# A new table of durations and delays for the list scheduler of a one-core decoder trunk

## The chip, the cores and the metric

One core of one Trainium2 chip runs the whole program in one launch. The metric is the device time of an execution in microseconds (us). Each time belongs to a run; the profile is that of one execution.

## The reference, cut to what matters

Two layers work on 256 tokens of width 1024, all in float32. Each layer adds four results to the residual `h`:

```
h += 0.5 * SwiGLU_1(rms(h))                          # width 2816
h += W_out [ A | B | C ](rms(h) @ W_in)
     # A: gated DeltaNet, 4 heads x 128: short causal conv on q/k/v, per-head decay, chunks
     #    t_inv = triangular_solve(eye + lower, eye); u = t_inv (v beta); w = t_inv (k beta exp(gc))
     # B: dilated sliding-window attention, 4 heads x 64;  C: chunked causal spatial gating
h += CrossAttn(rms(h), rms(mem))                     # 4 heads, 256 memory tokens
h += 0.5 * SwiGLU_2(rms(h))
```

After the second layer one more RMS norm gives the output. What is computed, and by which instructions, is the same before and after the change; only their order differs.

## The kernel before, in words

The function `trunk` (L421) does not issue instructions. It describes them, through small wrapper classes (`Tensor`, `Scalar`, `Vector`, `Queue`, L317 to L420), to an object of the class `Plan` (L136). Each wrapper gives `Plan.add` the engine, the operands and a rough duration. `Plan.schedule` (L191) then simulates the five engines with these durations. It always places the instruction that can start first; among those of one engine that can start at the same time it takes the one with the longest way to the end of the program ("rank"). `HOPS` are the delays from the end of an instruction on one engine to the start of one that depends on it on another. A tile gets one of the slots of its tag when its first instruction is placed, and for the tags in `KEEP` the last free slot is kept for the oldest waiting tile. `Plan.emit` (L298) issues the list, every instruction at L313. So each engine runs its instructions in the order that the simulation found, and the table of durations and delays sets that order. The loads of the weights keep the order of the program text.

The numerics are float32 by splitting: a weight piece `wr` [128, 1024] is rounded by ScalarE into `wh`, and VectorE (now and then GpSimd) writes the rest into `wl`. TensorE multiplies `wh` and `wl` with operands `X` (the gained residual) or `S`, into banks called `pg`; these matmuls have 512 or 256 columns and make up most of TensorE's work.

The small work stands in other tiles. `ps` are PSUM banks of everything that is no weight product. Statistics of a norm (`Stats`, `rsqrt`, `newton`): squares of the residual summed on GpSimd into `t`; TensorE sums over partitions (`ps<-one,t`); VectorE and GpSimd make the inverse root `rc` (`rv`, `rna`); TensorE spreads it over rows (`ps<-one,rch`), and VectorE stores it as `rb`. The mixing part (`mixing`) has the convolution in `xs` and `q`, the decays in `g8` (L830 to L848: three narrow matmuls with `g8` on one side, then per token tile four matmuls that spread it over 128 partitions), and the triangular inverse (L953 to L1003). For the inverse each of the two token tiles has a matrix in `uc` and its transposed blocks in `tc`. A level of it is: four 64x64 matmuls `ps<-tc,Mb`, two ScalarE copies into `Q`, four 64x64 matmuls `ps<-Q,uc`, then on VectorE two subtractions `tc<-tc,ps` and four block transposes `uc<-tc`, each over another group of 32 partitions. Four such levels follow each other, then a last one over `ng`, and two more products. The chain is long and each step is short, so the order decides what stands beside it.

Of the kernel before, what the change touches and what calls it, by code (L numbers as in the profile page):

```python
# [32 lines left out]
# columns of the constants that depend on shapes alone  # L33
# [10 lines left out]
# per-layer columns (small)  # L44
# [5 lines left out]
# per-layer columns (used in the mixing part)  # L50
# [8 lines left out]
class View:  # L59
    """A slice of a planned tile: where it lies, and how to take it from the real tile."""  # L60
# [75 lines left out]
class Plan:  # L136
    """Instructions in program order, placed on the engines by a list schedule (longest way to
    the end first) with rough durations in us, then issued in that order."""

    HOPS = {("ACT", "DVE"): 0.13, ("ACT", "GP"): 0.17, ("ACT", "PE"): 0.3, ("DVE", "ACT"): 0.13,  # L140
            ("DVE", "GP"): 0.16, ("DVE", "PE"): 0.7, ("GP", "DVE"): 0.06, ("GP", "PE"): 0.2,
            ("GP", "ACT"): 0.1, ("PE", "ACT"): 0.2, ("PE", "DVE"): 0.2,
            ("DVE", "DVE"): 0.13, ("ACT", "ACT"): 0.145, ("GP", "GP"): 0.1}
    DMA_ISSUE, DMA_DONE = 1.6, 1.8
    SLACK = 0.0
    KEEP = ("pg", "ps", "wh", "wl")  # their last free slot waits for the oldest tile
# [14 lines left out]
    def add(self, eng, method, args, kw, outs, ins, dur, table=None):  # L161
        i = len(self.ops)
        op = dict(i=i, eng=eng, method=method, args=args, kw=kw, dur=dur, table=table, prio=self.boost,
                  tiles=[], preds={}, succs=[])
# [21 lines left out]
    def hop(self, a, b):  # L186
        if a["eng"] == "DMA":
            return self.DMA_DONE
        return self.HOPS.get((a["eng"], b["eng"]), 0.0)

    def schedule(self):  # L191
        ops = self.ops
        for o in reversed(ops):
            o["tail"] = o["dur"] + max([ops[j]["tail"] + self.hop(o, ops[j]) for j in o["succs"]],
                                       default=0.0)
# [18 lines left out]
        dma_next, table = 0, None  # L214
# [6 lines left out]
        order, left = [], len(ops)  # L221

        def slot_time(o):
            """when slots for the tiles that o begins are free (None: not known yet)."""
            t = 0.0
            for x in o["tiles"]:
                if x.slot is None:
                    f = slots[x.tag]
                    best = min(f)
                    if x.tag in self.KEEP and queue[x.tag][0] is not x:  # L230
                        best = sorted(f)[1]
                    if best == float("inf"):
                        return None
                    t = max(t, best + (self.DMA_ISSUE if best and o["eng"] == "DMA" else 0.0))
            return t

        while left:
            best = None
            for e, lst in ready.items():
                if not lst:  # L240
                    continue
                if e == "DMA":
                    lst = [o for o in lst if o["i"] == dmas[dma_next]]
                cands = []
                for o in lst:
                    st = slot_time(o)
                    if st is not None:
                        cands.append((max(o["at"], st, free[e]), o))
# [4 lines left out]
                for t, o in cands:  # L253
                    if t > t0 + self.SLACK:
                        continue
                    k = o["rank"]
                    if e == "ACT" and o["table"] and table and o["table"] != table:
                        k -= 2.0
                    k = (k, -o["i"])
# [8 lines left out]
            dur = o["dur"]  # L268
            if e == "ACT" and o["table"] and o["table"] != table:
                dur += 1.28  # L270
                table = o["table"]
            if e == "DMA":
                dma_next += 1
            ready[e].remove(o)
            o["start"] = t
            end = free[e] = t + dur
            done = end + (self.DMA_DONE if e == "DMA" else 0.0)
            for x in o["tiles"]:
                if x.slot is None:
                    f = slots[x.tag]  # L280
                    x.slot = f.index(min(f))
# [3 lines left out]
                x.done = max(x.done, done)  # L285
                if not x.left:
                    slots[x.tag][x.slot] = x.done + 0.2
# [29 lines left out]
class Tensor:  # L317
# [3 lines left out]
    def matmul(self, o, lhsT, rhs, start, stop):  # L321
        n, m = o.free(), lhsT.shape[1]
        if lhsT.tile.dt == F32R and rhs.tile.dt == F32R:
            dur = max(n / 2.4, m / 1.2) / 1000 + 0.002
        else:
            dur = 2 * max(n / 1.2, m * 0.76) / 1000 + 0.004
        self.plan.add("PE", "matmul", (o,), dict(lhsT=lhsT, rhs=rhs, start=start, stop=stop),
                      [o], [lhsT, rhs], dur)

    def transpose(self, o, i, ident):  # L330
        self.plan.add("PE", "transpose", (o, i, ident), {}, [o], [i, ident], 0.11)


class Scalar:
    SETS = {AF.Exp: "exp", AF.Silu: "silu", AF.Tanh: None}

# [3 lines left out]
    def copy(self, o, i):  # L340
        self.plan.add("ACT", "copy", (o, i), {}, [o], [i], 0.09 + 0.83e-3 * o.free())

    def activation(self, o, i, f, **kw):
        n = o.free()
        dur = 0.09 + 0.83e-3 * n
        ins, outs = [i], [o]
        for k in ("scale", "bias"):
            if isinstance(kw.get(k), View):
                ins.append(kw[k])
                dur += 0.09  # L350
        if "accum_out" in kw:
            outs.append(kw["accum_out"])
            dur += 0.1
        table = "exp" if f in (AF.Exp, AF.Tanh) else "silu" if f == AF.Silu else None
        self.plan.add("ACT", "activation", (o, i, f), kw, outs, ins, dur, table)


class Vector:
# [3 lines left out]
    def _add(self, method, args, kw, outs, ins, fast=False, ap=0):  # L362
        n = max(outs[0].free(), ins[0].free()) if ins else outs[0].free()
        if self.eng == "GP":
            dur = 0.14 + 2.13e-3 * n
        else:
            dur = 0.068 + (0.52e-3 if fast else 1.04e-3) * n + 0.06 * ap
        if kw.get("op") == ALU.pow:
            dur = 0.3 + 0.165 * n
        if method == "memset":  # L370
            dur = 0.06 + 0.5e-3 * n
        if method == "reciprocal":
            dur = 0.07 + 6.3e-3 * n
        self.plan.add(self.eng, method, args, kw, outs, ins, dur)
# [35 lines left out]
class Queue:  # L410
# [3 lines left out]
    def dma_start(self, o, i):  # L414
# [3 lines left out]
        self.plan.add("DMA", "dma_start", (o, i), {}, [o], [i], max(n * 4 / 360e3, 0.1))  # L418


def trunk(tc, xT, memT, w, w2, ca_d, cb_d, sm_d, fin_d, lb_d, out):  # L421
    plan = Plan(tc)
    PE, ACT, DVE, GP, SY = Tensor(plan), Scalar(plan), Vector(plan, "DVE"), Vector(plan, "GP"), Queue(plan)
    with ExitStack() as ctx:
# [24 lines left out]
        # ---- residual and constants  # L449
# [46 lines left out]
        def wchunk(engs=(None, None), cut=1):  # L496
            """next weight chunk as two pieces of 1024 columns, each in two parts."""
# [11 lines left out]
        def mm3(o, wt, c, x, first, last):  # L509
            """o += W[:, c:c+128]^T x with W and x each in two parts."""  # L510
# [17 lines left out]
        def mm3x(o, x, t, wt, ws, first, last):  # L528
            """o += x[:, token tile t]^T W[:, ws]."""
# [16 lines left out]
        def mmp(o, a, i, sa, b, j, sb, first, last):  # L546
            """o += a[:, i, sa]^T b[:, j, sb] with both in two parts."""
# [4 lines left out]
        def gained(src, g, slot, dve=False):  # L552
            """two parts of src * g (g per partition)."""
# [19 lines left out]
        class Stats:  # L573
# [47 lines left out]
        class Norm:  # L621
            """operands and statistics of the next norm, one residual tile at a time."""
# [74 lines left out]
        def proj_add(ops, order, nxt):  # L697
            """h += W^T ops, two column tiles of W a chunk."""
# [10 lines left out]
        def pair(x, engs=(None, None)):  # L709
            """next chunk of two column tiles against x -> one bank [128, 2, 256]."""  # L710
# [7 lines left out]
        def xstat512(x):  # L718
            """two chunks of 4 k x 512 columns -> banks [tokens, 512] of both token tiles."""
# [11 lines left out]
        def xstat256(x, pieces=None, n=T):  # L731
            """8 k x n columns in two pieces -> banks [tokens, n] of both token tiles."""
# [48 lines left out]
        # ---- parallel mixing  # L781
        def mixing(l, norm, nxt, xm):
# [5 lines left out]
            # step sizes and decays  # L788
# [580 lines left out]
```

## Time and profile before

| | us |
|---|---|
| median of 3 runs | 1298.19 |
| lowest and highest run | 1297.84 and 1536.4 |
| span of the profiled execution | 1297.0 |
| TensorE (PE) busy in the span | 1257.6 |
| VectorE (DVE) busy | 985.8 |
| ScalarE (ACT) busy | 700.3 |
| GpSimd (POOL) busy | 267.3 |

The runs' time takes in a little more than the span: 0.8 to 1.2 us for the two lower runs. Of a matmul the trace shows a start and a modelled end, so two neighbours overlap; the distance from start to start tells what one costs. A float32 matmul that is not in the rounded form stands in the trace as two records. The number in square brackets behind a row is the time that the engine was idle ahead of it, and what ended it. "PEclk" is the granted clock of TensorE, 1.00 for 2.4 GHz and 0.50 for 1.2 GHz.

### The profile page before, as it was taken

The numbers are of one execution on the slowest core, as the hardware profiler recorded it, in microseconds if no ns is written. First come the engines' busy times: TensorE is split into PE (matmuls) and PEld (weight loads), VectorE is DVE, ScalarE is ACT, GpSimd is POOL, SyncE is SP. The second block draws the span as 40 slices with busy tenths as digits, with TensorE's granted clock in tenths as the row PEclk, the third lists the DMA queues.
The fourth block names the chain that finished last, engine by engine and source line by source line (L and its number), as shares of the span: only waits on it lengthen the run. The fifth ranks groups of instructions, "written<-read, shape, count | busy, mean of one in ns | idle before, by whom it ended". The sixth has DMA issues, their size and how long they took to land.

```text
span 1297.0 us, 21998 instructions
## 1 busy us (share of the span) xinstructions
PE 1257.6 (97%) x8376; PEld 1134.8 (87%) x8376; DVE 985.8 (76%) x1645; ACT 700.3 (54%) x1208; POOL 267.3 (21%) x281
## 2 busy tenths in 40 slices
PE   6999999899999999999999999989999999999997
PEld 5888889888999988888988888988989989888886
DVE  7777887997776777777777787779976767777764
ACT  5655645556544555555455664464564454565542
POOL 4000443603250230001200001435034305000021
PEclk9999999999999999999999999989999999999998
DMA  6556564323445345555555565532235453455551
GB/s 216 190 184 218 206 226 150 111 82 109 156 171 184 114 165 193 195 179 194 189 172 187 185 215 207 202 115 98 82 105 194 168 178 120 171 187 195 187 196 72
DMA packets 60873, 216.26 MB, mean 167 GB/s; under 512 B 7136, under 2 KB 7520, under 8 KB 60640
## 3 DMA queue, kind: packets, MB, share of 16 engines
q1 hardware_dynamic: 60768, 214.86, 48.5%
q8 instruction: 66, 1.08, 0.3%
q14 instruction: 39, 0.32, 0.1%
HBM read 213.78 MB, written 1.05 MB: 166 GB/s over the span
## 4 chain that ended last, share of the span: by engine, by line
PE 85%; DVE 8%; issue 3%; POOL 2%; ACT 1%; DMA 0%; POOLq 0%; DVEq 0%; SPq 0%; ACTq 0%
PE pg L313 78%; PE ps L313 8%; DVE wl L313 2%; DVE S L313 2%; POOL t L313 1%; DVE q L313 1%; ACT S L313 1%; DVE X L313 1%; ACT wh L313 1%; DVE tc L313 0%; DVE rna L313 0%; DVE ab L313 0%; DVE uc L313 0%; DMA one<-xT 0%; DVE po L313 0%
## 5 line engine op out<-in xcount | busy, mean ns | idle before, releaser
L313 PE MATMUL pg<-X,wh 128*128 128x512 f32 (+1 forms) x2240 | 642.4, 356 | 8.4 <-DVE X L313 8.4
L313 DVE TENSOR_TENSOR wl<-wr,wh 128x1024 fp32r<-128x1024 f32 (+1 forms) x386 | 483.3, 1260 | 194.4 <-ACT wh L313 190.1
L313 ACT CAST wh<-wr 128x1024 fp32r<-128x1024 f32 (+2 forms) x398 | 413.0, 1045 | 386.1 <-PE pg L313 227.2
L313 PE MATMUL pg<-X,wl 128*128 128x256 f32 x1824 | 484.7, 284 | 1.4 <-DVE wl L313 1.4
L313 PEld LDWEIGHTS pg<-X,wh 128*128 128x128 f32 x2240 | 384.4, 190 | 55.0 <-ACT wh L313 7.1
L313 PE MATMUL pg<-S,wh 128*128 128x256 f32 (+1 forms) x1560 | 383.5, 326 | 0.0
L313 PEld LDWEIGHTS pg<-X,wl 128*128 128x128 f32 x1824 | 345.4, 189 | 20.7 <-DVE wl L313 3.1
L313 PE MATMUL pg<-S,wl 128*128 128x256 f32 x1088 | 300.2, 281 | 1.3 <-DVE wl L313 1.3
L313 PEld LDWEIGHTS pg<-S,wh 128*128 128x128 f32 x1560 | 258.8, 188 | 24.7
L313 PEld LDWEIGHTS pg<-S,wl 128*128 128x128 f32 x1088 | 204.7, 188 | 4.3 <-DVE wl L313 1.8
L313 POOL TENSOR_TENSOR t<-one 128x256 f32<-128x256 f32 x70 | 55.2, 790 | 641.2 <-DVE one L313 635.9
L313 POOL TENSOR_TENSOR t<-t,t 128x256 f32<-128x256 f32 x68 | 89.7, 1320 | 4.7
L313 DVE TENSOR_TENSOR t<-t,pg 128x256 f32<-128x256 f32 x204 | 83.0, 414 | 5.9 <-ACT t L313 5.9
L313 ACT COPY t<-pg 128x256 f32<-128x256 f32 x204 | 73.4, 367 | 23.6 <-PE pg L313 21.4
L313 ACT ACTIVATE t<-t 128x256 f32<-128x256 f32 x88 | 36.7, 418 | 52.5 <-DVE t L313 52.4
L313 DVE SCALAR_TENSOR_TENSOR X<-one,one,X 128x256 fp32r<-128x256 f32 x64 | 55.9, 879 | 0.0
L313 PE MATMUL ps<-S,S 128*128 128x256 f32 (+4 forms) x384 | 51.2, 288 | 2.1 <-ACT S L313 1.2
L313 DVE TENSOR_TENSOR S<-t,S 128x256 fp32r<-128x256 f32 x88 | 37.0, 423 | 20.3 <-ACT S L313 20.3
L313 DVE TENSOR_TENSOR t<-t,rbh 128x256 f32<-128x256 f32 x116 | 49.6, 429 | 1.8 <-POOL t L313 0.2
L313 PEld LDWEIGHTS ps<-S,S 128*128 128x128 f32 (+2 forms) x384 | 44.4, 178 | 6.1 <-ACT S L313 1.7
L313 ACT CAST S<-t 128x256 fp32r<-128x256 f32 x88 | 35.0, 407 | 27.3 <-DVE t L313 27.3
L313 PE MATMUL pg<-wh,X 128*128 128x264 f32 (+2 forms) x192 | 45.4, 321 | 0.0
(178 smaller groups left out, 1011.8 us busy)
## 6 DMA issues: line engine op xcount, KB each, us to landing
wr<-w SPq DMA_DIRECT2D x390, 512.0 KB, 3.3
wr<-w SPq DMA_DIRECT2D x4, 528.0 KB, 3.3
S<-memT SPq DMA_DIRECT2D x8, 256.0 KB, 6.5
lb<-lb SPq DMA_DIRECT2D x2, 704.0 KB, 4.7
one<-cb SPq DMA_DIRECT2D x1, 1248.0 KB, 7.1
one<-xT SPq DMA_DIRECT2D x4, 256.0 KB, 5.1
wr<-w SPq DMA_DIRECT2D x4, 256.0 KB, 5.3
out<-S SPq DMA_DIRECT2D x3, 256.0 KB, 2.4
```

Source lines behind the costliest of these rows:

```text
L313: getattr(self.engines[o["eng"]], o["method"])(*[real(a) for a in o["args"]], **{k: real(a) for k, a in o["kw"].items()})
```

## The change

The scheduler's table is replaced. Delays between engines become shorter, above all to TensorE; the time that an engine is occupied (`dur`) and the time until the result can be read (`lat`) are two numbers; TensorE's kinds of matmul carry a cost of switching from one to the other; VectorE and GpSimd exclude each other in the simulation where both read two operands from the SBUF; the tag `t` joins `KEEP`; and the way to the end counts `lat` and the delay instead of the duration. The core of the diff:

```diff
-    HOPS = {("ACT", "DVE"): 0.13, ("ACT", "GP"): 0.17, ("ACT", "PE"): 0.3, ("DVE", "ACT"): 0.13,
-            ("DVE", "GP"): 0.16, ("DVE", "PE"): 0.7, ("GP", "DVE"): 0.06, ("GP", "PE"): 0.2,
...
-    KEEP = ("pg", "ps", "wh", "wl")  # their last free slot waits for the oldest tile
+    HOPS = {("PE", "ACT"): 0.037, ("PE", "DVE"): 0.037, ("ACT", "PE"): 0.054, ("DVE", "PE"): 0.054,
+            ("GP", "PE"): 0.054, ("ACT", "GP"): 0.079, ("DVE", "GP"): 0.079, ("GP", "GP"): 0.079,
+            ("PE", "PE"): -0.2}
+    HOP, ISSUE, FLIGHT, FEED = 0.034, 0.47, 1.75, 385e3
+    KEEP = ("pg", "ps", "wh", "wl", "t")
...
+                        if o["kind"] == "2":
+                            t = max(t, lock["GP" if e == "DVE" else "DVE"])
...
         if lhsT.tile.dt == F32R and rhs.tile.dt == F32R:
-            dur = max(n / 2.4, m / 1.2) / 1000 + 0.002
+            kind, dur = "r", max(0.4525e-3 * n, m / 1.2e3) + 0.0025
+            lat = 0.165 + 0.4525e-3 * n
...
     def copy(self, o, i):
-        self.plan.add("ACT", "copy", (o, i), {}, [o], [i], 0.09 + 0.83e-3 * o.free())
+        lat = (0.153 if i.tile.psum else 0.193) + 0.835e-3 * o.free()
+        self.plan.add("ACT", "copy", (o, i), {}, [o], [i], lat - 0.095, lat)
...
         if self.eng == "GP":
-            dur = 0.14 + 2.13e-3 * n
+            lat, over = 0.19 + 1.67e-3 * n, 0.04
+            if n >= 1024:
+                lat = 2.38
         else:
-            dur = 0.068 + (0.52e-3 if fast else 1.04e-3) * n + 0.06 * ap
+            lat, over = (0.155 if mem else 0.145) + (0.52e-3 if fast else 1.042e-3) * n + 0.06 * ap, 0.08
+            two |= fast and n > 64
...
+        self.plan.add(self.eng, method, args, kw, outs, ins, lat - over, lat,
+                      kind="2" if two or (self.eng == "GP" and views) else None)
```

Three places show what it moves. In names such as `ps_488_2565` the middle number is the tile's number in the program text, the same before and after; the last one tells when the tile was first used.

Place 1, TensorE around the decays `g8` in the first layer, before:

```order
L313 MATMUL pg_523_2458<-X_405_1975,wl_522_2439 128x256
L313 MATMUL ps_582_2558<-q_493_2338 128x128
L313 MATMUL ps_582_2558<-q_495_2346 128x128
L313 MATMUL ps_582_2558<-q_504_2435 128x128
L313 MATMUL ps_582_2558<-q_506_2444 128x128
L313 MATMUL ps_488_2565<-one9_11_1360,g8_484_2556 128x128 x4
L313 MATMUL ps_485_2572<-g8_484_2556,one9_11_1360 128x8
```

The same products after:

```order
L355 MATMUL pg_534_2561<-X_433_2129,wl_530_2509 128x256
L355 MATMUL pg_545_2574<-X_355_1737,wl_541_2581 128x256
L355 MATMUL ps_485_2599<-g8_484_2592,one9_11_1331 128x8
L355 MATMUL ps_485_2599<-g8_484_2592,one9_11_1331 128x4 x2
L355 MATMUL pg_545_2574<-X_366_1745,wh_540_2563 128x256 x2
...
L355 MATMUL pg_545_2574<-X_422_2039,wh_540_2563 128x256 x2
L355 MATMUL ps_488_2623<-one9_11_1331,g8_484_2592 128x128 x4
```

Before, the products with `g8` follow the transposes `ps_582` with no weight product between; after, the rest of `pg_523`, `pg_534` and the start of `pg_545` stand ahead of them, 23.6 us of matmuls by the spacing of their kinds.

Place 2, VectorE in the triangular inverse of the first layer (`tc_576`, `uc_575` are of the first token tile, `tc_586`, `uc_585` of the second), before:

```order
L313 TENSOR_TENSOR tc_576_77<-tc_576_77,ps_592_2828 64x4x32 x2
L313 STREAM_TRANSPOSE uc_575_2733<-tc_576_77 32x4x32 x4
L313 SCALAR_TENSOR_TENSOR q_547_2823<-xs_546_2378,one6_6_65,q_547_2823 128x256
...
L313 TENSOR_TENSOR wl_666_2901<-wr_664_2700,wh_665_2864 128x1024
L313 TENSOR_TENSOR tc_576_77<-tc_576_77,ps_598_2891 64x4x32 x2
L313 STREAM_TRANSPOSE uc_575_2733<-tc_576_77 32x4x32 x4
```

And after:

```order
L355 TENSOR_TENSOR tc_576_77<-tc_576_77,ps_592_3262 64x4x32 x2
L355 STREAM_TRANSPOSE uc_575_3103<-tc_576_77 32x4x32 x4
L355 TENSOR_TENSOR tc_586_85<-tc_586_85,ps_595_3268 64x4x32 x2
L355 STREAM_TRANSPOSE uc_585_3140<-tc_586_85 32x4x32 x4
L355 TENSOR_TENSOR qnqa_569_3270<-qnqa_569_3270,qrq_568_3247 128x8
L355 TENSOR_TENSOR S_722_3173<-S_722_3173,S_721_3162 128x512
L355 TENSOR_TENSOR tc_576_77<-tc_576_77,ps_598_3304 64x4x32 x2
L355 STREAM_TRANSPOSE uc_575_3103<-tc_576_77 32x4x32 x4
```

Before, the two token tiles' levels were spread between convolution and weight work; after, they alternate and stand nearly back to back. From `ps_592` to the last transposes of `uc_585` VectorE has 56 instructions of the chain's own (16 subtractions, 36 block transposes, 4 copies) and 13 others. On TensorE the same stretch holds 20 groups of four 64x64 matmuls and, between them, 17 matmuls of 512 columns with few others; before, the groups stood between the products `pg_556`, `pg_534`, `pg_670` and others of the projection. The second layer looks the same, with 24.7 us of VectorE work by the spacing of its kinds. Over the whole program the changes from a 64x64 group to another kind of product or back fall from 82 to 63.

Place 3, TensorE around the statistics of the second FFN's norm in the first layer (`ps_1037`), before:

```order
L313 MATMUL pg_1027_5312<-X_1016_5290,wh_1022_5238 128x512
L313 MATMUL pg_1027_5312<-X_1016_5290,wl_1023_5255 128x256
L313 MATMUL pg_1027_5312<-X_1019_5325,wl_1023_5255 128x256
L313 MATMUL ps_1037_5341<-one5_5_146,t_981_5061 128x1 x2
L313 MATMUL pg_1035_5344<-X_980_5066,wh_1030_5314 128x512
L313 MATMUL pg_1028_5348<-X_980_5066,wh_1025_5276 128x512
```

After:

```order
L355 MATMUL pg_1027_5314<-X_1019_5326,wl_1023_5257 128x256
L355 MATMUL pg_1035_5342<-X_980_5064,wh_1030_5316 128x512
L355 MATMUL pg_1035_5342<-X_980_5064,wl_1031_5329 128x256
L355 MATMUL pg_1035_5342<-X_983_5101,wh_1030_5316 128x512
L355 MATMUL pg_1027_5314<-X_1019_5326,wh_1022_5240 128x512
L355 MATMUL pg_1035_5342<-X_983_5101,wl_1031_5329 128x256
L355 MATMUL ps_1037_5349<-one5_5_120,t_981_5059 128x1 x2
```

Five weight products more stand ahead of the statistics after. The other norms' statistics move in the same way.

Beside these places, the transposes of the DeltaNet output (`ps_757`, `ps_760`, and `ps_2135`, `ps_2138` in the second layer) stand between pieces of `pg_769` (and its like) after, where they followed each other before. ScalarE loads a function table 14 times in place of 11. The order of the loads on SyncE is unchanged, and so is the end of the program.

## Rows read from the trace of the kernel before

**Rows 1.** The page: busy time, share of the span and instructions of each engine.
```profile
PE 1257.6 (97%) x8376; PEld 1134.8 (87%) x8376; DVE 985.8 (76%) x1645; ACT 700.3 (54%) x1208; POOL 267.3 (21%) x281
```

**Rows 2.** The waits of TensorE: us in total, times, longest.
```profile
PE pg L313 <- DVE X L313: 8.4, 3, 6.9
PE pg L313 <- DVE wl L313: 3.9, 6, 1.2
PE ps L313 <- DVE rch L313: 3.8, 3, 1.6
PE ps L313 <- POOL t L313: 3.5, 7, 1.1
PE ps L313 <- DVE S L313: 3.5, 6, 0.9
...
PE ps L313 <- DVE tc L313: 1.3, 2, 0.7
...
PE ps L313 <- POOL Mb L313: 0.9, 2, 0.7
```

**Rows 3.** Windows: length; PE, PEld, DVE, ACT, POOL busy (instructions); PEclk, DMA share, GB/s.
```profile
230.00:234.00 4.00, 1.74 (x16) 1.57 (x15) 3.79 (x12) 1.31 (x3) 2.64 (x2) 1.00 0.46 155
260.00:280.00 20.00, 20.00 (x198) 17.47 (x196) 19.03 (x54) 10.25 (x25) 2.47 (x8) 1.00 0.24 80
868.00:870.00 2.00, 2.00 (x13) 2.00 (x11) 1.12 (x2) 1.52 (x2) 1.20 (x1) 0.54 0.46 180
870.00:874.00 4.00, 4.00 (x20) 4.00 (x20) 1.33 (x4) 2.11 (x7) 0.00 (x0) 0.50 0.02 4
874.00:876.00 2.00, 2.00 (x15) 2.00 (x14) 2.00 (x8) 1.78 (x4) 1.13 (x2) 0.75 0.00 0
```

**Rows 4.** Timeline of TensorE (start, duration) at the decays of each layer.
```profile
233.86 1.13 PE L313 MATMUL ps<-one,g 128*128 128x128 f32 x8 [2.27 <-issue]
...
867.51 1.02 PE L313 MATMUL ps<-one,g 128*128 128x128 f32 x6 [2.32 <-DVE g L313]
```

**Rows 5.** Timeline of TensorE: weight products of 512 and 256 columns in turn.
```profile
600.04 0.39 PE L313 MATMUL pg<-S,wh 128*128 128x512 f32 x1
600.27 0.28 PE L313 MATMUL pg<-S,wl 128*128 128x256 f32 x1
600.39 0.39 PE L313 MATMUL pg<-S,wh 128*128 128x512 f32 x1
```

**Rows 6.** Timelines of VectorE, GpSimd and TensorE around the first inverse root of the mixing part.
```profile
207.75 2.33 DVE L313 SCALAR_TENSOR_TENSOR rna<-rv,rch 128x2 f32<-128x2 f32 x1 [0.82 <-POOL rch L313]
...
207.69 2.37 POOL L313 TENSOR_TENSOR wl<-wr,wh 128x1024 fp32r<-128x1024 f32 x1
...
210.53 0.71 PE L313 MATMUL ps<-one,rch 128*128 128x128 f32 x4 [1.07 <-DVE rch L313]
```

**Rows 7.** Timeline of TensorE: one 64x64 group and the weight products behind it.
```profile
255.64 0.65 PE L313 MATMUL ps<-tc,Mb 128*64 128x64 f32 x8 [0.69 <-DVE tc L313]
256.22 0.38 PE L313 MATMUL pg<-X,wl 128*128 128x256 f32 x1
256.44 0.40 PE L313 MATMUL pg<-X,wh 128*128 128x256 f32 x2
```

**Rows 8.** Timelines of VectorE and ScalarE in the triangular inverse.
```profile
254.91 0.58 DVE L313 TENSOR_TENSOR tc<-tc,ps 64x128 f32<-64x128 f32 x2
255.52 1.25 DVE L313 STREAM_TRANSPOSE uc<-tc 32x128 f32<-32x128 f32 x4
256.81 0.64 DVE L313 SCALAR_TENSOR_TENSOR q<-xs,one,q 128x256 f32<-128x256 f32 x1
...
278.94 0.69 DVE L313 TENSOR_TENSOR S<-ps,beta 128x512 f32<-128x512 f32 x1
279.55 1.22 DVE L313 TENSOR_TENSOR wl<-wr,wh 128x1024 fp32r<-128x1024 f32 x1
...
256.94 1.28 ACT L313 ACT_TABLE_LOAD   x1
```

More of the change, by code (lines that the diff above doesn't have):

```diff
@@ L159, with add @@
     boost = 0.0
-    def add(self, eng, method, args, kw, outs, ins, dur, table=None):
+    def add(self, eng, method, args, kw, outs, ins, dur, lat, table=None, kind=None):
         i = len(self.ops)
-        op = dict(i=i, eng=eng, method=method, args=args, kw=kw, dur=dur, table=table, prio=self.boost,
-                  tiles=[], preds={}, succs=[])
+        op = dict(i=i, eng=eng, method=method, args=args, kw=kw, dur=dur, lat=lat, table=table, kind=kind,
+                  prio=self.boost, tiles=[], preds={}, succs=[])
         for views, wr in ((ins, False), (outs, True)):
@@ L213, in schedule @@
                     queue[x.tag].append(x)
-        dma_next, table = 0, None
+        dma_next, table, kind, feed = 0, None, None, 0.0
+        lock = {"DVE": 0.0, "GP": 0.0}
         dmas = [o["i"] for o in ops if o["eng"] == "DMA"]
@@ L221, in schedule @@
         order, left = [], len(ops)
+        turn = None
+        if fixed:
+            turn = {e: [o for o in fixed if o["eng"] == e] for e in self.engines}
+            place = {e: 0 for e in self.engines}
+            seq = {}
+            for o in fixed:
+                for x in o["tiles"]:
+                    if x not in seq.setdefault((x.tag, x.was), []):
+                        seq[x.tag, x.was].append(x)
         def slot_time(o):
@@ L228, in slot_time, with switch @@
                     f = slots[x.tag]
-                    best = min(f)
-                    if x.tag in self.KEEP and queue[x.tag][0] is not x:
-                        best = sorted(f)[1]
+                    if fixed:
+                        if seq[x.tag, x.was][0] is not x:
+                            return None
+                        best = f[x.was]
+                    else:
+                        best = min(f)
+                        if x.tag in self.KEEP and queue[x.tag][0] is not x:
+                            best = sorted(f)[1]
                     if best == float("inf"):
                         return None
-                    t = max(t, best + (self.DMA_ISSUE if best and o["eng"] == "DMA" else 0.0))
+                    t = max(t, best)
             return t
+        def switch(o):
+            k = o["kind"]
+            if kind == "r" and k[0] == "f":
+                return 0.091
+            if kind and kind[0] == "f" and k == "r":
+                return 0.2 if kind == "fs" else 0.023
+            return 0.0
         while left:
@@ L243, in schedule @@
                     lst = [o for o in lst if o["i"] == dmas[dma_next]]
+                elif fixed:
+                    lst = [o for o in lst if o is turn[e][place[e]]]
                 cands = []
@@ L258, in schedule @@
                         k -= 2.0
+                    if e == "PE" and switch(o):
+                        k -= self.HOLD
                     k = (k, -o["i"])
@@ L273, in schedule @@
                 dma_next += 1
+                feed = max(feed, t + self.FLIGHT) + lat
+                lat = feed - t
+            if e == "PE":
+                t += switch(o)
+                kind = o["kind"]
+            if o["kind"] == "2":
+                lock[e] = t + dur
             ready[e].remove(o)
+            if fixed:
+                place[e] += 1
             o["start"] = t
-            end = free[e] = t + dur
-            done = end + (self.DMA_DONE if e == "DMA" else 0.0)
+            free[e] = t + dur
+            end = o["end"] = t + lat
             for x in o["tiles"]:
@@ L280, in schedule @@
                     f = slots[x.tag]
-                    x.slot = f.index(min(f))
+                    x.slot = x.was if fixed else f.index(min(f))
                     f[x.slot] = float("inf")
@@ L362, in _add @@
     def _add(self, method, args, kw, outs, ins, fast=False, ap=0):
-        n = max(outs[0].free(), ins[0].free()) if ins else outs[0].free()
+        views = [v for v in ins if isinstance(v, View)]
+        n = max(outs[0].free(), views[0].free()) if views else outs[0].free()
+        mem = [v for v in views if not v.tile.psum and v.free() > 1]
+        two = len(mem) > 1
         if self.eng == "GP":
-            dur = 0.14 + 2.13e-3 * n
-        else:
-            dur = 0.068 + (0.52e-3 if fast else 1.04e-3) * n + 0.06 * ap
+            lat, over = 0.19 + 1.67e-3 * n, 0.04
+            if n >= 1024:
+                lat = 2.38
+        else:
+            lat, over = (0.155 if mem else 0.145) + (0.52e-3 if fast else 1.042e-3) * n + 0.06 * ap, 0.08
+            two |= fast and n > 64
         if kw.get("op") == ALU.pow:
-            dur = 0.3 + 0.165 * n
+            lat = 0.38 + 0.165 * n
         if method == "memset":
-            dur = 0.06 + 0.5e-3 * n
+            lat, over, two = 0.1 + 0.8e-3 * n, 0.0, False
         if method == "reciprocal":
-            dur = 0.07 + 6.3e-3 * n
-        self.plan.add(self.eng, method, args, kw, outs, ins, dur)
+            lat = 0.14 + 6.3e-3 * n
+        self.plan.add(self.eng, method, args, kw, outs, ins, lat - over, lat,
+                      kind="2" if two or (self.eng == "GP" and views) else None)
     def tensor_tensor(self, o, a, b, op):
```

54 lines of the change are left out of this document (27 added, 27 removed).

## The prediction

> **What bounds the kernel now.** I read the page first: TensorE is busy for 1257.6 of 1297.0 us and no other engine comes near [rows 1]. So 39.4 us are all that TensorE is idle, and the time can only fall by what its waits, its changes between kinds of product, or a low clock give back. The list of its waits comes next [rows 2]. The 8.4 us for `X` are the start of the program (6.9 of it before the first matmul) and the tail is unchanged, so neither is in play. What remains in play is short and spread out: 3.9 us for `wl`, 3.8 for `rch`, 3.5 for `t` on GpSimd, 3.5 for `S`, 2.2 for `tc` and `Mb`, and the two waits for the decays, 2.27 and 2.32 [rows 4]. The windows [rows 3] then show two things that the list of waits does not. First, in the mixing part VectorE is nearly full, 19.03 of 20 us at 260 to 280 us, while TensorE is at 20.00: the two engines are close to each other there, so an order that bunches VectorE's work makes TensorE wait. Second, after the idle time ahead of 867.51 TensorE runs at a granted clock of 0.54, 0.50 and 0.75 until 876 us, though it is busy throughout.
>
> **The sum.** It is made against the profiled execution, whose span of 1297.0 stands 1.2 us below the median of the runs; I add the sum to the median.
>
> *Decays (place 1).* Before, TensorE had nothing to do until VectorE had finished the small chain to `g8` (VectorE 3.79 of 4 us busy at 230 to 234 [rows 3]). After, 23.6 us of weight products stand there, against 17.1 us of VectorE work up to `g8`. Both waits go: 2.27 + 2.32 = -4.6. The cover would have to shrink by 6.5 us before any wait comes back.
>
> *Clock in the second layer.* With that idle time gone the half-clock stretch has no cause. At the granted clocks it lost 2 x 0.46 + 4 x 0.50 + 2 x 0.25 = 3.4 us of TensorE's full speed [rows 3]: -3.4. In the first layer the same wait left the clock at 1.00, so nothing is to be had there.
>
> *Statistics (place 3).* Five products more stand ahead of the sums: three of 512 columns at 0.23 us (600.04 to 600.27) and two of 256 at 0.12 (600.27 to 600.39) [rows 5], together 0.93. The wait at this place was the longest, 1.1, of the seven that make 3.5 us [rows 2]. The others moved alike, and four fifths of the sum should go: -2.8, with ends of 0 (the products wait for their own `wh`) and -3.5.
>
> *First inverse root of the mixing part.* At 207.75 a VectorE operation on two columns took 2.33 us, exactly while GpSimd formed a `wl` for 2.37 us [rows 6]; TensorE then waited 1.07 for `rch`. After, that `wl` comes behind the operation, because the slot of its `wh` comes free later. But fewer products cover the root too (14 of `pg_460` and one other, before 22), so I keep 0.3 us of the wait. Two layers, 2 x 0.8: -1.6, with ends 0 and -2.2.
>
> *Output transposes.* They stand between weight products after; of the six waits for `S`, 3.5 us with 0.9 as the longest [rows 2], the four at these transposes go: -2.5, with ends 0 and -3.5. The rest, in cross attention, keeps its order.
>
> *`wl`.* Of 3.9 us [rows 2] I take -1.4: the places ahead of the mixing part and behind it have more products in front of them. The ends are 0 and -3.9; the loads on SyncE are issued in the same order, so nothing new queues there.
>
> *Changes of kind.* A 256-column product after a 64x64 group costs 0.22 us (256.22 to 256.44) where it costs 0.12 elsewhere [rows 5, 7]; I take 0.09 to 0.10 for each direction. There are 19 fewer changes: -1.8.
>
> *Triangular inverse (place 2).* This is the term on the other side, and the largest. On VectorE one level of one token tile takes 254.91 to 256.81 = 1.90 us: two subtractions at 0.31 and four transposes at 0.32 [rows 8]. The new order has eight of these (15.2), four more transposes (1.3), four copies (an estimate of 0.8) and 13 other instructions: one `wl` at 1.2, four 512-wide at 0.6 (278.94 to 279.55), the rest narrow, some 1.8; 5.4 in all. Together 22.7 us. TensorE has for the same stretch 20 groups of 64x64 at 0.47 (8 records; 255.64 to 256.22, less one change) = 9.4, 17 products at 0.23 = 3.9, some 0.8 of other work and about 24 changes = 2.2: 16.3 us. The two alternating tiles keep VectorE busy all through, so TensorE waits for the difference, 6.4 us; in the second layer 24.7 against 19.0, 5.7. That is +12.1 in many pieces of 0.3 to 0.7 us, and 2.2 us of `tc` and `Mb` waits before go into it: +9.9. The ends for a layer are 0 (VectorE runs ahead, or the products next in line fill in) and 16 (the tiles do not alternate, and the 9.4 us of groups come on top).
>
> The Trainium skill ("VectorE: DVE Perf Modes", section "Two Vector instructions with no wait between them") says that an instruction whose first input from a memory starts in another group of 32 partitions than that of the instruction before starts only when all earlier ones have finished. The four transposes of a tile go over four such groups, and they take 0.32 us from start to start, no less than the 0.30 that each lasts [rows 8]. The new table gives VectorE 0.08 us of overlap on every instruction, 0.21 for such a transpose; by the table the wait would be about 1 us a layer and the sum some 10 us lower; by the rule the order cannot change the 0.32, and the sum stands.
>
> *The rest.* ScalarE loads three more tables at 1.28 us [rows 8]. It is 54% busy [rows 1], and its casts stay ahead of VectorE's `wl`; I cost them at nothing. One falls into the chain of the first layer ahead of a copy to `Q`; uncovered it costs 1.28.
>
> Sum: -4.6 - 3.4 - 2.8 - 1.6 - 2.5 - 1.4 - 1.8 + 9.9 = -8.2, so 1298.2 - 8.2 = **1290.0**. 2% of this kernel, about what a measurement tells from no change, is 26 us; the forecast is a third of it.
>
> **Rivals.**
>
> *The new table is right in the chain as well.* For it: the other entries come near what the trace shows (a 512-wide product 0.23, a `wl` 1.2). Against it: the 1.90 us for a level, where the table has 1.2. Then the 12.1 are not paid: 1298.2 - 20.3 = 1278, and down to 1270 if the remaining `wl`, `X` and cross-attention waits shrink as well. Chance 0.17.
>
> *The chain takes the clock down.* For it: in the second layer an idle time of 2.32 us left eight microseconds at 0.50 to 0.75 [rows 3, 4]. Against it: in the first layer 2.27 us of idle, in a window with 1.74 us busy of 4, left it at 1.00, and the chain's gaps are short and its TensorE 72% busy (16.3 of 22.7). A fall that lasts as long as that one costs 3.4 a layer; at half clock throughout, the chain's 16.3 us become 32.6 and outlast VectorE by 9.9. Two layers: +6.8 to +19.8 on the forecast, 1297 to 1310; I take 1303. It is slower than before as soon as the two layers together lose 8.2. Chance 0.16.
>
> The Trainium skill ("TensorE: Matmul & The Clock Gate", Part 1) has the gate follow how busy TensorE has recently been; that speaks for this rival without saying that 72% is too little, and the trace shows both outcomes after almost the same idle time.
>
> *VectorE sets the length of the mixing part in any order.* For it: 19.03 of 20 us [rows 3]. Against it: VectorE is 76% busy over the program, and some of its work can move to the FFN. Then what is gained at the decays and the output transposes returns as other waits, and only the terms outside (statistics, clock, `wl`) are left, about half of them: 1298.2 - 4 = 1294. Chance 0.17.
>
> **How the numbers follow.** The forecast has 0.50. Its own spread, from the ends of the chain and the small terms, is about 1283 to 1297. The range for 8 in 10 takes in most of the first rival and the lower half of the second: 1274 to 1305. Under 1272.2 lies the low end of the first rival, 0.06; above 1324.2 only a chain that loses its clock and its alternation together, 0.03; within 2%: 0.91.
>
> **What would show it.** Right: no wait for `g` near 234 and 868 us; a clock of 1.00 at 868 to 876; `t` waits under 1 us in sum; and a cluster of `tc` and `Q` waits, about 6 us, in the stretch of the 64x64 groups, with VectorE at nearly 100% there and the transposes still 0.32 us apart. Wrong: no such cluster (first rival), a clock under 0.9 in it (second), or the same total of waits under other names (third).

## The result, and the profile after

The changed kernel takes 1316.8 us (median of 4 runs, 1315.5 to 1320.5) where the kernel before takes 1298.6: the ratio is 1.0142, with a 95% interval of 1.0125 to 1.016. The forecast was 1290.0 and the range ended at 1305. The kernel became slower by 18 us, and that is well clear of the noise. One of the four runs of the kernel before, at 1536.4 us, was in a slow state; the ratio is taken without it.

The page of the changed kernel, busy time by engine, answers to [rows 1]:

```profile
span 1314.8 us, 21994 instructions
PE 1266.0 (96%) x8376; PEld 1136.2 (86%) x8376; DVE 982.5 (75%) x1645; ACT 703.7 (54%) x1212; POOL 271.4 (21%) x281
```

TensorE, VectorE and GpSimd run as many instructions as before; ScalarE has four more, all loads of a function table (20 in this trace, 16 in that of the kernel before, where the prediction counted three more). VectorE is busy no longer than before. Of the 17.8 us of span, 9.4 are idle time of TensorE (48.8 in place of 39.4) and 8.4 are time in which it counts as busy. The start of the statistics matmuls (`ps<-one,t`, 128x1) in both timelines tells in which stage they come in:

| stage ends at the statistics of | before, us | after, us | stage changed by |
|---|---|---|---|
| mixing, layer 1 | 206.1 | 208.8 | +2.7 |
| cross attention, layer 1 | 379.7 | 388.8 | +6.4 |
| second FFN, layer 1 | 466.1 | 474.1 | -1.1 |
| first FFN, layer 2 | 653.4 | 661.9 | +0.5 |
| mixing, layer 2 | 839.7 | 849.9 | +1.7 |
| cross attention, layer 2 | 1016.1 | 1034.0 | +7.7 |
| second FFN, layer 2 | 1102.1 | 1119.2 | -0.8 |
| end of the span | 1297.0 | 1314.8 | +0.7 |

The two mixing parts have 14.1 of the 17.8 us. What the 2.7 us ahead of the first of them are was not followed up. The waits of TensorE after (us in total, times, longest; those of 1 us and more) answer to [rows 2]:

```profile
PE pg L355 <- DVE wl L355: 10.9, 11, 4.7
PE pg L355 <- DVE X L355: 9.0, 6, 7.1
PE ps L355 <- DVE tc L355: 6.6, 12, 0.9
PE ps L355 <- ACT q L355: 5.1, 4, 1.6
PE ps L355 <- DVE S L355: 3.1, 5, 1.0
PE ps L355 <- DVE rch L355: 1.6, 1, 1.6
PE ps L355 <- DVE t L355: 1.4, 1, 1.4
PE pg L355 <- ACT wh L355: 1.4, 3, 0.8
PE ps L355 <- DVE qvk L355: 1.0, 1, 1.0
```

Against [rows 2]: the waits for `t` on GpSimd (3.5) and for the decays (4.6) are gone, `rch` fell from 3.8 to 1.6. New or grown are `wl` (3.9 to 10.9), `tc` (1.3, with `Mb` 2.2, to 6.6), `q` (0.8 to 5.1), `wh` and `qvk`. The list holds only idle time.

Of the 8.4 us for which TensorE counts as busy, a lower clock explains 1.2 (worked out below). The rest, some 7 us, is no idle time in the profile: the matmuls start further apart. The list of the weight loads (PEld), each of which stands just ahead of its matmul, points to where such time comes from. Their waits for `wl`, in the kernel before, the changed one, and two of the experiments below (`e8_before_hop` and `e11_after_start`):

```profile
PEld pg L313 <- DVE wl L313: 6.3, 8, 2.0
PEld pg L355 <- DVE wl L355: 19.1, 32, 5.0
PEld pg L313 <- DVE wl L313: 14.8, 22, 2.0
PEld pg L357 <- DVE wl L357: 6.2, 8, 1.8
```

The weight loads waited for `wl` 8 times before and 32 times after. Part of this is covered by matmuls still under way, so these totals can't be added to the others; that they make up the 7 us is likely, not shown.

The three large waits of TensorE's list look like this. First `wl`, in the second layer. Timelines of TensorE and VectorE:

```profile
915.74 2.19 PE L355 MATMUL ps<-S,S 64*128 64x256 f32 x22
922.64 0.58 PE L355 MATMUL pg<-X,wl 128*128 128x256 f32 x1 [4.72 <-DVE wl L355]
...
916.24 1.46 DVE L355 TENSOR_TENSOR uc<-mc,one 128x256 f32<-128x256 f32 x2
917.62 1.28 DVE L355 TENSOR_TENSOR uc<-one,uc 128x256 f32<-128x256 f32 x2
918.82 2.51 DVE L355 STREAM_TRANSPOSE tc<-uc 32x128 f32<-32x128 f32 x8
921.36 1.22 DVE L355 TENSOR_TENSOR wl<-wr,wh 128x1024 fp32r<-128x1024 f32 x1
```

VectorE prepares the inverse of both token tiles in one piece, 5.1 us, and only then forms the `wl` that TensorE needs. TensorE starts 0.06 us after that `wl` ends (921.36 + 1.22 = 922.58). So the short delay of the new table, 0.054 us, is what this row shows; the two rows of TensorE below give 0.05 as well. What it does not have is room, that is, time in the plan for a late operand. How late VectorE is can be estimated in part: by the diff the plan charges 0.155 + 1.042e-3 x 256 - 0.08 = 0.34 us for each of the four `uc` steps and 0.21 for each of the eight transposes, 3.0 us in all, where the rows show 5.1. So some 2 us of this wait can come from charges that are too small. That the matmul was planned for the moment when `wl` was due is a reading; the trace holds no planned times.

The windows behind that wait (columns as in [rows 3]) show the second price, the granted clock:

```profile
922.00:923.00 1.00, 0.36 (x1) 0.36 (x2) 1.00 (x3) 0.00 (x0) 0.00 (x0) 0.74 0.00 0
923.00:925.00 2.00, 2.00 (x11) 2.00 (x11) 2.00 (x7) 0.69 (x2) 0.00 (x0) 0.50 0.66 201
925.00:927.00 2.00, 2.00 (x15) 1.99 (x14) 1.96 (x4) 1.01 (x4) 0.00 (x0) 0.78 0.15 61
```

That is 2 x 0.50 + 2 x 0.22 and a little at 922, some 1.5 us.

Second, `q`, in the first layer. Timelines of ScalarE, VectorE, GpSimd and TensorE:

```profile
222.44 1.28 ACT L355 ACT_TABLE_LOAD   x1
223.73 0.21 ACT L355 ACTIVATE ex<-ab 128x8 f32<-128x8 f32 x1
223.96 1.28 ACT L355 ACT_TABLE_LOAD   x1
225.25 0.42 ACT L355 ACTIVATE q<-q 128x256 f32<-128x256 f32 x1
226.27 0.91 ACT L355 ACTIVATE q<-xs,one 128x256 f32<-128x256 f32 x2 [0.60 <-DVE xs L355]
...
223.32 2.36 DVE L355 TENSOR_SCALAR at<-at 128x8 f32<-128x8 f32 x1
...
225.82 0.74 DVE L355 TENSOR_TENSOR xs<-pg,rbh 128x256 f32<-128x256 f32 x2
...
223.24 2.37 POOL L355 TENSOR_TENSOR wl<-wr,wh 128x1024 fp32r<-128x1024 f32 x1
...
225.72 0.71 PE L355 MATMUL ps<-q 128*128 128x128 f32 x4 [1.60 <-ACT q L355]
...
227.53 0.71 PE L355 MATMUL ps<-q 128*128 128x128 f32 x4 [0.99 <-ACT q L355]
```

TensorE has been given the products of `q` (`ps<-q`) right behind ScalarE's step. Ahead of the first wait ScalarE works without a pause from 222.44 us on, 2.56 us of it in two table loads. Ahead of the second it waits 0.60 us for `xs`, which VectorE forms only when the drawn-out `at<-at` (2.36 us beside GpSimd's `wl`) is over. The same pair of waits stands in the second layer at 867 us (1.61 and 0.85), and there the clock falls again.

Third, `tc`: a level of the inverse on VectorE and TensorE, which answers to [rows 8].

```profile
302.28 0.58 DVE L355 TENSOR_TENSOR tc<-tc,ps 64x128 f32<-64x128 f32 x2
302.89 1.25 DVE L355 STREAM_TRANSPOSE uc<-tc 32x128 f32<-32x128 f32 x4
...
302.91 0.68 PE L355 MATMUL ps<-tc,Mb 128*64 128x64 f32 x8 [0.88 <-DVE tc L355]
```

The four transposes still take 1.25 us, as before, and TensorE waits for the subtraction.

### The profile page after: what moved, and what is told of

The parts are those of the page before. It is cut to its first block, busy times and chain, and to the rows that moved or that the text cites. A ratio compares the mean times of both kernels' runs of the same rounds, so it can differ in the third digit from the quotient of the medians.

```text
span 1314.8 us, 21994 instructions
## 1 busy us (share of the span) xinstructions
PE 1266.0 (96%) x8376; PEld 1136.2 (86%) x8376; DVE 982.5 (75%) x1645; ACT 703.7 (54%) x1212; POOL 271.4 (21%) x281
## 3 DMA queue, kind: packets, MB, share of 16 engines
HBM read 213.78 MB, written 1.05 MB: 163 GB/s over the span
## 4 chain that ended last, share of the span: by engine, by line
PE 80%; DVE 12%; issue 3%; ACT 2%; DMA 1%; POOL 1%; POOLq 0%; DVEq 0%; SPq 0%; ACTq 0%
PE pg L355 75%; PE ps L355 5%; DVE wl L355 3%; DVE S L355 2%; DVE uc L355 2%; ACT wh L355 1%; DVE q L355 1%; DVE tc L355 1%; DVE X L355 1%; ACT t L355 1%; DVE at L355 0%; DMA S<-memT 0%; ACT q L355 0%; DVE t L355 0%; DMA one<-xT 0%
## 5 line engine op out<-in xcount | busy, mean ns | idle before, releaser
L355 PEld LDWEIGHTS pg<-X,wh 128*128 128x128 f32 x2240 | 389.2, 190 | 60.4 <-ACT wh L355 9.5
L355 POOL TENSOR_TENSOR t<-one 128x256 f32<-128x256 f32 x70 | 60.6, 867 | 648.9 <-DVE one L355 643.9
L355 PE MATMUL pg<-wh,X 128*128 128x256 f32 (+2 forms) x192 | 50.2, 334 | 0.3
```

The costliest lines, as they stand in the source:

```text
L355: getattr(self.engines[o["eng"]], o["method"])(*[real(a) for a in o["args"]], **{k: real(a) for k, a in o["kw"].items()})
```

## The experiments

All times are medians; the kernel before took 1298.4 to 1299.5 beside them, and each ratio is against it.

**The late start or the small charges.** In the new order TensorE reaches the inverse at 291 us, 41 us later than before. In the plan one PSUM bank (`ps_635`) is opened for transposes of `k` as soon as the first two heads are there, and filled only 44 us later (226.3 to 270.1 us in the timeline), while the matmuls that lead to the inverse find no bank. That was my first theory; the rival was the small charges that the forecast had counted on.

`e1_bank` holds those transposes, and the like ones of `v`, back in the plan:

```diff
+        if self.hold is not None:
+            op["preds"][self.hold] = True
...
+            plan.hold = gate
             ps = hmm(lambda o, i: PE.transpose(o, kT[i][:, 0:P], ident))
+            plan.hold = None
```

> The changed kernel, but in the plan the transposes that open the bank ps_635 (and its like of the second layer) wait for the first tiles of the triangular inverse. Bank theory (that bank is opened some 40 us too early and keeps the entry of the inverse off TensorE, so the inverse comes late and bunched): the inverse starts as early as before the change, the waits for tc fall from 6.6 us by the wait list to under 3, the 4.7 us wait for wl at 922 us goes, and the time falls from 1316.8 to about 1304. Table theory (the inverse is bunched because the new table charges its VectorE steps too little): the order of the inverse may move but it stays bunched, tc waits stay at 6 us or more, time 1313 to 1318.

Measured: 1318.4 (1.0155, 1.014 to 1.017). The inverse starts early, at 255 us, as meant, and no wait for `wl` is longer than 1.5 us any more. But the `tc` waits grow, and the time does not fall: as an account of the loss the bank theory falls. The waits of TensorE:

```profile
PE ps L357 <- DVE tc L357: 9.2, 12, 2.1
PE pg L357 <- DVE wl L357: 6.1, 10, 1.5
```

`wl` lost 4.8 us of waiting, but `tc` gained 2.6, and other waits took the rest. The table theory fits the waits; the time is 0.4 us above its range.

`e2_chaincost` gives the inverse's steps their measured durations:

```diff
+        if method == "transpose" or (self.eng == "DVE" and outs[0].tile.tag == "tc"):
+            lat, over = 0.35, 0.035
...
+        over = 0.0 if o.tile.tag == "Q" else 0.095
+        self.plan.add("ACT", "copy", (o, i), {}, [o], [i], lat - over, lat)
```

> The changed kernel with the inverse's steps charged as the trace shows them: 0.315 us for a subtraction or a transpose on VectorE, 0.26 for a copy to Q on ScalarE, in place of 0.21 and 0.17. Table theory: the scheduler now puts enough weight products beside the inverse, tc waits under 3 us, time about 1306. Bank theory: the inverse still starts at the same late place, tc waits 5 us or more, time 1312 to 1318.

Measured: 1310.6 (1.0097, 1.0082 to 1.0112), 6.2 us less than the changed kernel. No wait for `tc` is left in its list, and in the window of the inverse TensorE is full:

```profile
288.00:315.00 27.00, 27.00 (x250) 21.11 (x248) 24.08 (x73) 11.26 (x33) 5.71 (x11) 1.00 0.17 58
```

So this step of the forecast is right in kind: with the charges mended the waits for `tc` are gone. But 12 us of loss are left, and the 4.7 us wait for `wl` is still there (of the piece of VectorE's work ahead of it this edit mends the transposes, not the `uc` steps).

**The exclusion.** `e3_nolock` takes out the two lines by which VectorE and GpSimd exclude each other in the plan (`if o["kind"] == "2": t = max(t, lock[...])`).

> The changed kernel without the rule that VectorE and GpSimd exclude each other in the simulation. Bank theory: in this order the early bank does not arise, so the inverse starts early and the time falls to 1300 to 1306. Table theory: the inverse stays bunched, 1313 to 1318. A third theory, that the exclusion is right and worth much: more VectorE instructions stand beside GpSimd's and are drawn out, time above 1317.

Measured: 1332.1 (1.0264, 1.0249 to 1.0279). Both main theories miss; the third one holds as far as the number goes. Beside the other parts of the change the exclusion is worth some 15 us. The waits for GpSimd's `t` come back and grow:

```profile
PE ps L353 <- POOL t L353: 7.2, 7, 1.5
```

`e4_bank_lockall` is `e1_bank` with the exclusion widened to narrow instructions (`two |= fast`, without `and n > 64`).

> As e1_bank, and the exclusion also holds for VectorE's narrow fast instructions (128 x 8), of which one took 2.36 us beside a GpSimd wl at 223.3 us just ahead of the waits for q (5.1 us in the wait list). If that instruction causes the waits for q: they fall under 2 us, and the time is 3 us or more below e1_bank. If the two table loads of ScalarE cause them: they stay, and the time is within 1.5 us of e1_bank.

Measured: 1324.2 (1.0202, 1.0185 to 1.0219), 5.8 us above `e1_bank`. But the edit did not reach its aim: in this run too the narrow instruction stands beside a GpSimd `wl` of 2.38 us (223.26) and is drawn out.

```profile
223.33 2.37 DVE L357 TENSOR_SCALAR at<-at 128x8 f32<-128x8 f32 x1
```

So that the waits for `q` stay, at 5.6 us, tells nothing about its part in them. The rows of the changed kernel above tell more: the first wait of the pair has the two table loads ahead of it, the second the drawn-out instruction. That the time rises fits neither expectation. I read it as the spread between orders, below.

**The room ahead of TensorE.** The diff says it plainly: the delay from VectorE to TensorE falls from 0.7 to 0.054, and that from ScalarE from 0.3 to 0.054. The forecast has no term for it. A delay stands at two places in the scheduler: in the earliest start of what depends on an instruction, and in the way to the end, which sets the rank. The next three go out from `e2_chaincost` and set the old two delays at one place or both:

```diff
+    FAR = {("DVE", "PE"): 0.7, ("ACT", "PE"): 0.3}
...
+    def hop(self, a, b, far):
+        k = a["eng"], b["eng"]
+        return far.get(k) or self.HOPS.get(k, self.HOP)
...
+                q["at"] = max(q["at"], end + self.hop(o, q, self.FAR))
```

> As e2_chaincost (1310.6), and in the simulated start times the delay to TensorE is again that of before, 0.7 us from VectorE and 0.3 from ScalarE; the way to the end that sets the rank keeps the new ones. Margin theory (with a delay of 0.054 TensorE's work is placed right at the moment when its operand is planned to be ready, and any lateness on VectorE stops it; the long delay was room for that): the waits for wl, q and S of TensorE, 20.3 us in e2_chaincost, fall to about 10, time about 1299. Rank theory (what counts is that the long delay raised the rank of the narrow chains): no gain, 1308 to 1312.

Measured: 1299.2 (1.0001, 0.9992 to 1.001). The waits for `wl`, `q` and `S` fall from 20.3 to 10.6 us. Both are as the margin theory had it.

> As e2_chaincost, with the long delays of before only in the way to the end that sets the rank. Rank theory: about 1300. Margin theory: 1308 to 1312.

Measured: 1319.8 (1.0162, 1.0144 to 1.018), slower than either theory had it.

> As e2_chaincost, with the long delays of before in start times and rank. Margin theory: as e5_start, about 1299. Rank theory: as e6_rank. If both count: below both, 1293 to 1297, under the kernel before.

Measured: 1304.5 (1.0042, 1.0025 to 1.0059). That fits none of the expectations; the margin theory's 1299 is the nearest. Room in the start times gives 11.4 us back (`e5_start`); the same delays in the rank give nothing, here even a loss. `e8_before_hop` turns the question round and makes this one part of the change in the kernel before:

```diff
-    HOPS = {("ACT", "DVE"): 0.13, ("ACT", "GP"): 0.17, ("ACT", "PE"): 0.3, ("DVE", "ACT"): 0.13,
-            ("DVE", "GP"): 0.16, ("DVE", "PE"): 0.7, ("GP", "DVE"): 0.06, ("GP", "PE"): 0.2,
+    HOPS = {("ACT", "DVE"): 0.13, ("ACT", "GP"): 0.17, ("ACT", "PE"): 0.054, ("DVE", "ACT"): 0.13,
+            ("DVE", "GP"): 0.16, ("DVE", "PE"): 0.054, ("GP", "DVE"): 0.06, ("GP", "PE"): 0.2,
```

> The kernel before with one edit: the delays to TensorE from VectorE (0.7) and ScalarE (0.3) are 0.054, as in the change, in start times and rank. Margin theory: TensorE waits more, 1304 to 1312. If the delays do not matter and the loss lies in the other entries of the table: 1296 to 1301.

Measured: 1316.1 (1.0135, 1.0119 to 1.015): these two numbers alone make the old kernel as slow as the whole change, and slower than either theory had it. The step is a little larger than in the change: the old durations lack some 0.08 us that the new `lat` has (0.068 against 0.145 to 0.155 in the diff), so this plan has TensorE start a little before VectorE's result is there. The weight loads wait for `wl` 22 times in place of 8 (above). TensorE's own waits are of the same kind, many and short:

```profile
PE pg L313 <- DVE wl L313: 8.4, 13, 1.2
PE ps L313 <- DVE tc L313: 4.4, 5, 2.4
PE ps L313 <- POOL t L313: 3.6, 5, 1.1
PE ps L313 <- ACT t L313: 3.0, 2, 1.5
```

**How much, where, and is it luck.** `e9_half` and `e10_more` are `e5_start` with 0.35 and 0.15, and with 1.05 and 0.45.

> As e5_start (1299.2) with half the delays in the start times: 0.35 us from VectorE, 0.15 from ScalarE. Margin theory: between e2_chaincost (1310.6, at 0.054) and e5_start, 1301 to 1307. If e5_start owed its time to one lucky order: anywhere, as likely above 1310 as below 1300.

Measured: 1304.4 (1.0037, 1.0023 to 1.0052).

> As e5_start with one and a half times the delays: 1.05 and 0.45 us. Margin theory: fewer waits for wl, q and S still, but the plan keeps TensorE's narrow work back longer; 1294 to 1302. Luck: anywhere up to 1315.

Measured: 1306.1 (1.0048, 1.0032 to 1.0063). With `e2_chaincost` and `e5_start` the row is 1310.6, 1304.4, 1299.2, 1306.1 for 0.054, 0.35, 0.7 and 1.05 us. It falls with the room as the theory has it up to 0.7, and rises beyond, outside what I expected of the margin theory; the luck theory allows that last value.

`e11_after_start` is the changed kernel, wrong charges and all, with the `FAR` of above in the start times alone.

> The changed kernel with one edit: in the start times the delays to TensorE are 0.7 from VectorE and 0.3 from ScalarE again; the inverse's steps keep the change's too small charges. If the charges cost on top of the margin (e2_chaincost gave 6.2 back): about 1305, with tc waits of 4 us or more. If the margin covers the charges too: 1298 to 1301.

Measured: 1298.2 (0.9992, 0.9983 to 1.0001). All of the 18 us are back. The weight loads wait for `wl` 8 times again (above). The waits that grew have shrunk, and those for `q` are gone from the list, of which these are the first six:

```profile
PE pg L357 <- DVE X L357: 7.9, 3, 7.1
PE ps L357 <- DVE tc L357: 4.4, 8, 0.9
PE pg L357 <- DVE wl L357: 3.3, 5, 1.4
PE ps L357 <- DVE S L357: 2.5, 4, 0.9
PE ps L357 <- POOL Mb L357: 2.2, 2, 1.3
PE ps L357 <- ACT S L357: 2.0, 2, 1.0
```

`e12_before_rank` is the kernel before with 0.054 in the way to the end alone.

> The kernel before with the short delays to TensorE (0.054) in the way to the end alone; start times keep 0.7 and 0.3. Margin theory: the loss of e8_before_hop (1316.1) comes from the start times, so this one stays at 1296 to 1302. If the rank made e8_before_hop slow: 1310 to 1318.

Measured: 1300.0 (1.001, 1.0001 to 1.002). The weight loads wait for `wl` 8 times, as before. The rank is not it, from this side either.

**Which of the two delays.** `e13_dve_only` and `e14_act_only` are `e11_after_start` with one delay each (`FAR = {("DVE", "PE"): 0.7}` and `{("ACT", "PE"): 0.3}`).

> As e11_after_start (1298.2) with the delay from VectorE alone (0.7 in the start times; ScalarE's stays at 0.054). Margin theory with VectorE as the late engine: 1297 to 1302. If ScalarE's delay matters as much: 1305 to 1312.

Measured: 1304.5 (1.0043, 1.0027 to 1.006), between the two expectations.

> As e11_after_start with the delay from ScalarE alone (0.3 in the start times; VectorE's stays at 0.054). Margin theory with VectorE as the late engine: 1312 to 1318, with the inverse late and its tc waits as in the changed kernel. If ScalarE's delay matters as much: 1303 to 1310.

Measured: 1315.7 (1.0125, 1.011 to 1.014), with the inverse late and `q` at 5.1 us as in the changed kernel. VectorE's delay gives 12.3 us back, ScalarE's alone 1.1, both together 18.6. VectorE is the engine whose lateness counts most. With its delay alone the weight loads wait for `wl` 14 times, with ScalarE's alone 39 times. The other 5 us come only with both; they are no more than the spread between orders, below.

One companion of the loss was not tested by itself: the four more table loads. The trace of every run without room in the start times towards VectorE's results has 20 of them, save `e3_nolock`; that of every run with such room has 16. `e8_before_hop` shows that the two delays are enough to bring them, and `e3_nolock`, the slowest of all with its 16, that a loss does not need them.

`e15_x_charge` mends one more charge on top of `e11_after_start` (VectorE's step to `X`).

> As e11_after_start, and VectorE's step that writes X is charged 0.83 us, as the trace shows it beside GpSimd, in place of 0.40. If the charges left wrong cost time where the room is back: 1294 to 1297, under both kernels. If the room covers them: 1297 to 1300.

Measured: 1304.7 (1.0044, 1.0029 to 1.0059). A truer number, and 6.5 us worse, outside both expectations. Like `e4_bank_lockall`, `e6_rank`, `e7_both` and `e10_more` this shows how much one order differs from the next when any number of the table changes: 5 to 9 us, each time upward. The 17 to 19 us of `e8_before_hop` and `e11_after_start` are about twice the largest of these; the difference between `e5_start` and `e11_after_start`, and the last few us of either, can't be told from a lucky order. No version beat the kernel before by more than its interval.

## Why the prediction was wrong, step by step

The step that failed is one that the sum did not have: what the shorter delays to TensorE do. It was taken at nothing, and it costs 17.4 us when it is the only change (`e8_before_hop`). The terms one by one:

*Decays: right.* Neither wait (2.27, 2.32) is in the list any more.

*Clock in the second layer: wrong.* The forecast had -3.4 because "the half-clock stretch has no cause". The cause moved: after the waits for `q` at 867 us the windows read

```profile
868.00:869.00 1.00, 0.48 (x2) 0.48 (x3) 1.00 (x2) 1.00 (x4) 0.00 (x0) 0.50 0.90 340
869.00:871.00 2.00, 2.00 (x11) 2.00 (x11) 2.00 (x6) 1.98 (x4) 0.00 (x0) 0.50 0.46 137
871.00:873.00 2.00, 2.00 (x12) 2.00 (x11) 2.00 (x8) 1.97 (x3) 0.20 (x2) 0.50 0.44 174
873.00:875.00 2.00, 2.00 (x12) 2.00 (x12) 1.55 (x11) 1.70 (x5) 0.00 (x0) 0.58 0.38 133
```

which is 3.1 us for the 3.4 of [rows 3], and the 1.5 us at 922 come on top: +1.2 in place of -3.4. The second rival had the clock fall in the inverses. It did not fall there (both windows have 1.00):

```profile
291.00:317.00 26.00, 22.04 (x216) 16.66 (x213) 22.84 (x72) 11.22 (x33) 6.73 (x12) 1.00 0.16 56
936.00:955.00 19.00, 15.50 (x149) 11.66 (x147) 17.76 (x56) 7.60 (x23) 4.36 (x4) 1.00 0.09 31
```

*Statistics: right.* -3.5 for -2.8. *First inverse root: right.* -2.2 for -1.6.

*Output transposes: wrong.* -0.4 in place of -2.5: the weight products stand between them now, and the first still waits 1.03 us at 341 us.

*`wl`: wrong in sign.* "The places ahead of the mixing part and behind it have more products in front of them" gave -1.4; measured +7.0, of which 4.7 is the one wait at 922.64. Behind it stand the weight loads' waits for `wl`, 32 in place of 8.

*Changes of kind: open.* No run separates the -1.8 from the rest.

*Triangular inverse: right in kind, too large.* The gross term was +12.1; the list has 6.6 for `tc` after, and mending the charges gave 6.2 back (`e2_chaincost`). In the two windows above TensorE is idle for 4.0 and 3.5 us, where the forecast had 6.4 and 5.7. The walk took VectorE as full all through; it is busy for 22.84 of 26 and 17.76 of 19 us. The list shows waits of up to 0.9 us, 12 of them, as it foresaw, but not between all levels. The rule that the Trainium skill ("VectorE: DVE Perf Modes", section "Two Vector instructions with no wait between them") has for the transposes held: 1.25 us for four, before and after.

*The other rivals: neither came true.* The first had no waits for `tc`, and they are 6.6 us. The third had the mixing parts as long in any order, and they became 6.4 and 7.7 us longer.

*The rest: a step that was missing.* "I cost them at nothing" covered ScalarE's table loads; two of them stand ahead of `q`, and the waits for `q` went from 0.8 to 5.1 us. Above all no term asked what the two shortened delays do. I took each new order as if every engine would reach its instructions at the times of the old trace, and summed the places where the order was visibly better or worse. Two numbers in the kernel before cost 17.4 us (`e8_before_hop`), and the same two put back, in the start times alone, give all of the loss back (`e11_after_start`). So the old 0.7 us was not a wrong measure that happened to do no harm. I read it as room: with it TensorE meets its operands ready more often. The waits of the weight loads for `wl` (8, 32, 22 and 8 times in the kernel before, the changed one, `e8_before_hop` and `e11_after_start`) bear this out. It does not cover each wait in its place, since 0.7 us is less than the 4.7 of the longest; the order as a whole becomes another one.

What stays open: what makes single orders differ by 5 to 9 us, and what the 7 us of TensorE's busy time consist of.

## What to carry to other kernels

A truer number in a table of durations need not make a better order when the scheduler has no other allowance for lateness: an offset that looks wrong may be the only room in the plan. Before such numbers are corrected, put the room back as a number of its own, in the start times and not in the ranks, towards the engine that must not stop. More of it is not always better: 1.05 us gave 1306.1 where 0.7 gave 1299.2. And when a change replaces a whole table, the first experiment is one entry of it alone in the old kernel.

## What was not expected of the hardware

A VectorE instruction on 128 x 8 elements took 2.36 us beside a GpSimd instruction of 2.37 us (223.32 and 223.24, above), and one on 128 x 2 took 2.33 us in [rows 6]. The same `at<-at` took 0.11 us in the kernel before (227.93), where no GpSimd `wl` ran beside it. And the clock fell to 0.50 after two waits of 1.61 and 0.85 us at 867 us with 0.8 us of matmuls between, while in the first layer the like pair at 226 us (1.60 and 0.99) left it at 1.00; what tells the two apart no run here shows.
